# The sample's chunk of two pairs of heads as one unit of half A's RWKV recurrence

## Chip, core and metric

The kernel runs on one core of one Trainium2 chip. The metric is the device time of one execution in microseconds (us), the median of several runs. The engines are PE (TensorE, with PEld for its weight loads), DVE (VectorE), ACT (ScalarE), POOL (GpSimd) and SP (SyncE), whose queue issues nearly all DMAs of this kernel. Each engine works through its own instruction stream in order and waits on semaphores.

## What is computed

One inference step of a two-layer encoder trunk over 1024 prompt frames and 64 sample frames, in fp32. Layer 0 has a mixer of two kinds: RWKV-7 time mixing (8 heads of 64) and gated linear attention, GLA (4 heads); layer 1 has chunk-band attention; each layer has a SwiGLU. Prompt and sample go through the same weights, with states of their own. The change is in the RWKV mixer:

```
xs = pa + (prev - pa) * mu                      # token shift of the projected rows
r, k, v, xw, xa, xg = split(xs)
w = -softplus(-(w0 + tanh(xw) @ w2)) - 0.5;  decay = exp(-exp(w))
a = sigmoid(a0 + xa @ a2);  g = sigmoid(xg) @ g2
kk = normalised k * k_k;  k = k * (1 + (a - 1) * k_a)
S = S * w_t - (S kk_t) (kk_t a_t)^T + v_t k_t^T;  o_t = S r_t     # per head, frame after frame
y = (groupnorm(o) * ln_w + ln_b + sum(r k r_k) v) * g
...
mix = concat(ya, yb) @ w_out_mix
```

## The kernel before

**Halves and stages.** The 1088 frames are cut in two: half A is the first 384 prompt frames and the 64 sample frames (448 columns), half B the other 640 prompt frames. The program text goes: input projection of A for the RWKV part (`inproj_rwkv(0)`); recurrence of A, interleaved with the GLA units of A and the projection of A for the GLA part; loading of B's input (`load_xt(1)`) and B's projections (`inproj_gla(1)`, `inproj_rwkv(1)`); loading of A's mixer outputs (`load_xt(0, yg_d)`) and of the residual rows (`load_acc`, line 797); four steps of B's recurrence; A's output projection (`proj`, through `tsg`, evacuations in lines 825 to 829) with its layer norm (lines 887 to 905); the rest of B's recurrence; the first SwiGLU of A (`ffn(0, 0)`). Every GEMM of fp32 operands is made of three passes over high and low parts (lines 124 to 126, and 135 to 138), the parts split off by ACT (`wh`, `xh`) and by DVE or POOL (`wl`, `xl`).

**The recurrence.** It is worked in chunks of 64 frames. A unit holds one pair of heads (128 partitions) and `n` chunks. Half A has 16 units: first four for the sample, of one chunk each (pairs 0 to 3, 64 columns), and then 12 of two chunks each (three times four pairs, 128 columns). Half B has 20 units of two chunks. A unit goes through five stages: `rw1` (loads of `rkv`, `xg`, `rsb`; three small matmuls into `pa`; decay and keys), `rw1b` (`pb`: the chunk's 64x64 matrices; `lab`, line 487; the transposes into `pt`), `rw2` (the inverse of a triangular matrix: `lab` goes to DRAM, its 16x16 diagonal blocks come back as `lt` with `8*n` partitions, 15 pairs of tiny DVE instructions in lines 549 and 551 solve them, and the result goes through DRAM to `tt` and `t0`; then two levels of matmuls in `pz`), `rw3` (chunk after chunk: state and output, eight matmuls each in their dependence) and `rw4` (transposition, gate, store of `y` to `yg_d`, line 654). The generator `rwkv` lets five units be in flight, one in each stage. `pa`, `pb` and `pt` share one PSUM bank, `pz` has one; `lt`, `x16` and `bbk` have one buffer each.

**Order.** The instructions are ordered when the program is built: a planner simulates all engines with a cost model, takes among the ready instructions the one written earliest, and gives out buffers. The stream of each engine is therefore a mixture of recurrence, GEMM and filler, fixed beforehand; where a real duration differs from the planner's, the engine waits at the head of its stream.

**What the tail of A's recurrence feeds.** `load_xt(0, yg_d)` loads eight row blocks `yraw` (line 214), four from GLA and four from RWKV, and splits them (lines 215 and 216) into the tiles `xh`, `xl` of half A. These tiles lend part of their space to half B's input while B's projection runs (`xt_tiles_in`). The `yraw` buffers and the projection's temporary tiles are given up before `acc`, the residual rows, is loaded; `acc` lies in that space. Filler work, such as `cache_setup` (`cv`, `ck`, `cvh`, lines 1126 to 1132, casts by line 113) and the weight casts of line 101, stands in the same streams.

Of the kernel before, what the change touches and what calls it, by code (L numbers as in the profile page):

```python
# [10 lines left out]
F32 = mybir.dt.float32  # L11
F32R = mybir.dt.float32r
U8 = mybir.dt.uint8
AF = mybir.ActivationFunctionType
# [5 lines left out]
PA = 384  # L20
NA, NB = PA + 64, 1024 - PA
NM = max(NA, NB)
SMP = PA
# [60 lines left out]
class Kern:  # L84
# [324 lines left out]
        eng.tensor_tensor(dst, src.unsqueeze(2).to_broadcast([128, m, 2, 64]),  # L409
                          self.bd3.unsqueeze(1).to_broadcast([128, m, 2, 64]), op=ALU.mult)  # L410

    def rw1(self, sp, p, n, g0):

        nc, V, A, G, T = self.nc, self.V, self.A, self.G, self.T
        W = 64 * n
        u = SimpleNamespace(p=p, n=n)
        pc = slice(128 * p, 128 * p + 128)
# [7 lines left out]
        gs = slice(g0, g0 + W)  # L425
        rkv = sp.tile([128, 3, W], F32, tag="rkv", name="rkv", bufs=3)
        nc.sync.dma_start(rkv, self.rkv_d[:, p, :, gs].rearrange("a p t -> p a t"))
# [4 lines left out]
        for h in range(2):  # L432
            src = self.rs_d[2 * p + h : 2 * p + h + 1, gs]
            nc.sync.dma_start(rsb[QH[h]], bass.AP(tensor=src.tensor, offset=src.offset, ap=[[0, 64], [1, W]]))

        pa = self.sbank("pa")
        T.matmul(pa[:, 0:W], self.w2z[:, pc], xg[:, 0, :], start=True, stop=True)
        T.matmul(pa[:, W : 2 * W], self.a2z[:, pc], xg[:, 0, :], start=True, stop=True)
        T.matmul(pa[:, 2 * W : 3 * W], self.g2[:, pc], xg[:, 1, :], start=True, stop=True)
        th = st("th", bufs=2)  # L440
        A.activation(th, pa[:, 0:W], AF.Tanh, bias=self.w0h[:, p : p + 1], scale=0.5)
        tha = st("tha")
        A.activation(tha, pa[:, W : 2 * W], AF.Tanh, bias=self.a0h[:, p : p + 1], scale=0.5)
        u.gt = st("gt", bufs=5)
        A.copy(u.gt, pa[:, 2 * W : 3 * W])
        kkn = st("kkn")
        V.scalar_tensor_tensor(kkn, k, self.kk[:, p : p + 1], rsb, op0=ALU.mult, op1=ALU.mult)
# [17 lines left out]
        G.tensor_scalar(tha, tha, self.kah[:, p : p + 1], self.kah1[:, p : p + 1], op0=ALU.mult, op1=ALU.add)  # L465
        G.tensor_tensor(tha, tha, k, op=ALU.mult)
        V.scalar_tensor_tensor(th, r, self.rk[:, p : p + 1], tha, op0=ALU.mult, op1=ALU.mult)
        G.tensor_tensor(bk[:, :, 1, :], ch(tha), ch(enb), op=ALU.mult)
        u.v, u.th, u.eb3, u.ar, u.bk = v, th, eb3, ar, bk
        return u  # L470

    def rw1b(self, sp, u):

        V, A, G, T, p, n = self.V, self.A, self.G, self.T, u.p, u.n
# [123 lines left out]

    def rw3(self, sp, u, S):

        V, A, G, T, p, n = self.V, self.A, self.G, self.T, u.p, u.n
# [36 lines left out]
        for h in range(2):  # L638
# [4 lines left out]
        return S2  # L643

    def rw4(self, sp, u, y0):

        A, G, T, p, W = self.A, self.G, self.T, u.p, 64 * u.n
# [3 lines left out]
        A.activation(y, py[:, 0:W], AF.Identity, scale=self.lnw[:, p : p + 1], bias=self.lnb[:, p : p + 1])  # L651
        G.tensor_tensor(y, y, u.bon, op=ALU.add)
        G.tensor_tensor(y, y, u.gt, op=ALU.mult)
        self.nc.sync.dma_start(self.yg_d[p, :, y0 : y0 + W], y)

    def rwkv(self, hf, sp, n, src, S):

        units = [(p, n, 64 * c, 0) for c in range(0, (PA, NB)[hf] // 64, n) for p in range(4)]
        if hf == 0:
            units = [(p, 1, SMP, 1) for p in range(4)] + units  # L660
            S += [self.state(sp, p, self.a["wkv0"]) for p in range(4)]
        else:
            S += [self.state(sp, p, src) for p in range(4)]
        st = {}
        def one(i):
            p, m, c0, smp = units[i]
            st[i] = self.rw1(sp, p, m, self.base[hf] + c0)

        def three(i):
            p, m, c0, smp = units[i]  # L670
            S[p] = self.rw3(sp, st[i], S[p])
            if smp:
                self.wkv_out(sp, S[p], self.a["s_wkv"][2 * p : 2 * p + 2])
                S[p] = self.state(sp, p, src)
            elif hf == 0 and c0 == PA - 64 * n:
                self.nc.sync.dma_start(self.wkv_d[p].rearrange("(h k) v -> k h v", h=2), S[p])
# [917 lines left out]
```

## Time and profile before

| what | value |
|---|---|
| median of 3 runs | 3114.89 us (3114.37 to 3117.97) |
| the profiled execution's own time | 3118.8 us |
| its span, first to last instruction | 3117.0 us |
| mean granted TensorE clock | 0.978 |
| half A's recurrence, first `lab` to last store of `y` | 100.2 to 551.4 us |
| half B's recurrence, last store of `y` | 1117.7 us |

The profile page gives busy time by engine, slices of the span, the chain of work that ended last and the costliest groups of instructions. The views behind it are asked by stretch (busy time of every engine between two times), by line or tile (count, durations, first and last start), by waits, and as a timeline. In a timeline a row reads: start, duration, engine, line, operation, output and inputs, shapes, count, and in square brackets the idle time of the engine before it and what ended that. A PE row's duration contains a modelled tail, so the distance of two starts tells more of the pace than the duration does.

### The profile page before, as it was taken

To read this page: it belongs to the slowest core of one execution; us is meant where nothing else is said; L and a number is where in the kernel's file an instruction comes from. 1 tells how busy PE (TensorE), PEld (TensorE's weight loads), DVE (VectorE), ACT (ScalarE), POOL (GpSimd) and SP (SyncE) were. 2 spreads that over 40 slices of the span, in tenths; PEclk is the share of its full clock that TensorE was granted. 3 is DMA by queue.
4 is the path that set the end of the run, shared out by engine and by line. 5 is a ranking of instruction groups with operands and counts; after the bars stand their busy time and mean duration, and the time that the engine had idled before them with its cause. 6 is when DMAs were issued, how large, how long until landed. Compare 5 with 4: busy or idle time off the path is not lost.

```text
span 3117.0 us, 50050 instructions
## 1 busy us (share of the span) xinstructions
PE 3007.7 (96%) x17468; PEld 2672.1 (86%) x17468; DVE 2025.6 (65%) x4941; ACT 1271.7 (41%) x2761; POOL 1363.4 (44%) x1489
## 2 busy tenths in 40 slices
PE   8999999899999999999999999999999989799998
PEld 7878888688888888798999898899999968799987
DVE  5687875879898764555554556245666668666567
ACT  4454554344444334243343132355444433333332
POOL 2354533444554234343342233245555556645444
PEclk9999999889999999999999999999999999999999
DMA  6553334533533238344443223865445443322122
GB/s 200 142 161 113 109 111 122 147 104 107 148 113 103 83 105 296 106 155 123 121 123 100 75 102 116 255 186 172 137 144 150 122 160 108 108 80 96 65 82 75
DMA packets 298492, 399.29 MB, mean 128 GB/s; under 512 B 125504, under 2 KB 218552, under 8 KB 298240
## 3 DMA queue, kind: packets, MB, share of 16 engines
q1 hardware_dynamic: 297088, 393.48, 41.0%
q8 instruction: 138, 2.26, 0.3%
q10 hardware_dynamic: 1152, 2.62, 0.2%
q14 instruction: 114, 0.93, 0.1%
HBM read 323.63 MB, written 75.51 MB: 128 GB/s over the span
## 4 chain that ended last, share of the span: by engine, by line
PE 78%; DMA 7%; DVE 7%; POOL 3%; issue 2%; ACT 2%; SPq 1%; POOLq 0%; ACTq 0%; DVEq 0%
PE gps L124 11%; PE gps L126 11%; PE gps L125 11%; PE gps L135 8%; PE gps L136 8%; PE gps L138 7%; PE gps L1066 2%; PE gps L1067 2%; PE gps L1068 2%; PE op L1329 2%; PE tp L1303 2%; PE sps L1287 1%; PE sps L1288 1%; PE ps L622 1%; DVE x L551 1%
## 5 line engine op out<-in xcount | busy, mean ns | idle before, releaser
L108 POOL TENSOR_TENSOR wl<-wr,wh 128x512 fp32r<-128x512 f32 (+2 forms) x297 | 522.9, 1763 | 655.5 <-ACT wh L101 602.3
L124 PE MATMUL gps<-xh,wh 128*128 128x320 f32 (+1 forms) x2188 | 746.4, 341 | 8.5 <-ACT xh L215 5.8
L125 PE MATMUL gps<-xl,wh 128*128 128x320 f32 (+1 forms) x2188 | 745.9, 341 | 0.6 <-DVE xl L216 0.6
L126 PE MATMUL gps<-xh,wl 128*128 128x320 f32 (+1 forms) x2188 | 745.1, 341 | 0.2
L101 ACT CAST wh<-wr 128x1024 fp32r<-128x1024 f32 x360 | 375.9, 1048 | 465.8 <-PE gps L125 136.5
L106 DVE TENSOR_TENSOR wl<-wr,wh 128x512 fp32r<-128x512 f32 (+2 forms) x297 | 288.8, 973 | 252.2 <-ACT wh L101 249.1
L124 PEld LDWEIGHTS gps<-xh,wh 128*128 128x128 f32 x2188 | 415.0, 190 | 30.1 <-ACT xh L215 5.8
L126 PEld LDWEIGHTS gps<-xh,wl 128*128 128x128 f32 x2188 | 414.5, 189 | 18.6 <-POOL wl L108 1.2
L125 PEld LDWEIGHTS gps<-xl,wh 128*128 128x128 f32 x2188 | 414.5, 189 | 18.3 <-DVE xl L216 1.0
L1298 POOL TENSOR_SCALAR s<-s,mx 128x640 f32<-128x640 f32 (+5 forms) x144 | 203.0, 1410 | 277.2 <-DVE mx L1297 250.4
L135 PE MATMUL gps<-wh,xh 128*128 128x512 f32 x661 | 263.1, 403 | 9.2 <-ACT wh L101 3.8
L138 PE MATMUL gps<-wh,xl 128*128 128x512 f32 x661 | 259.2, 399 | 6.6 <-DVE xl L216 6.1
L136 PE MATMUL gps<-wl,xh 128*128 128x512 f32 x661 | 264.2, 401 | 0.4 <-DVE wl L106 0.2
L135 PE MATMUL gps<-wh,hh 128*128 128x512 f32 x572 | 226.7, 398 | 3.8 <-ACT xh L113 3.5
L136 PE MATMUL gps<-wl,hh 128*128 128x512 f32 x572 | 226.9, 398 | 0.0
L827 DVE TENSOR_TENSOR acc<-acc,gps 128x512 f32<-128x512 f32 x216 | 143.5, 679 | 84.8 <-PE gps L138 82.3
L138 PE MATMUL gps<-wh,hl 128*128 128x512 f32 x484 | 189.6, 397 | 1.3 <-DVE hl L946 1.1
L549 DVE TENSOR_TENSOR t<-lt,x 16x48 f32<-16x48 f32 (+9 forms) x540 | 151.2, 280 | 35.6 <-DMA lt<-l_d 25.2
L1296 ACT ACTIVATE s<-s,mx 128x640 f32<-128x640 f32 (+5 forms) x144 | 96.4, 670 | 161.2 <-DVE mx L1295 151.7
L135 PEld LDWEIGHTS gps<-wh,xh 128*128 128x128 f32 x661 | 126.5, 192 | 39.9 <-ACT wh L101 6.4
L138 PEld LDWEIGHTS gps<-wh,xl 128*128 128x128 f32 x661 | 126.0, 191 | 35.4 <-DVE xl L216 7.0
L136 PEld LDWEIGHTS gps<-wl,xh 128*128 128x128 f32 x661 | 126.7, 192 | 30.2 <-DVE wl L106 2.0
(380 smaller groups left out, 6308.3 us busy)
## 6 DMA issues: line engine op xcount, KB each, us to landing
wr<-in_w_fi SPq DMA_DIRECT2D x176, 512.0 KB
wr<-in_w_fo SPq DMA_DIRECT2D x88, 512.0 KB
wr<-in_w_in SPq DMA_DIRECT2D x44, 512.0 KB
wr<-in_w_qk SPq DMA_DIRECT2D x32, 512.0 KB
wr<-in_w_o SPq DMA_DIRECT2D x24, 512.0 KB
qs<-qd SPq DMA_DIRECT2D x32, 320.0 KB
wr<-in_w_om SPq DMA_DIRECT2D x16, 512.0 KB
wr<-in_w_v SPq DMA_DIRECT2D x16, 512.0 KB
```

Source lines behind the costliest of these rows:

```text
L101: self.A.copy(hi, raw)
L106: self.V.tensor_tensor(lo[:, :h], raw[:, :h], hi[:, :h].bitcast(F32), op=ALU.subtract)
L108: self.G.tensor_tensor(lo[:, h:], raw[:, h:], hi[:, h:].bitcast(F32), op=ALU.subtract)
L124: self.T.matmul(ps, hi[:, kt, :], xh, start=(kt == 0), stop=False)
L125: self.T.matmul(ps, hi[:, kt, :], xl, start=False, stop=False)
L126: self.T.matmul(ps, lo[:, kt, :], xh, start=False, stop=(kt == nk - 1))
L135: self.T.matmul(ps, xh, wh, start=(i == 0), stop=False)
L136: self.T.matmul(ps, xh, wl, start=False, stop=(lo is None and i == n - 1))
L138: self.T.matmul(ps, cols(lo(kt)), wh, start=False, stop=(i == n - 1))
L549: V.tensor_tensor(tv, lt[:, j, w:16].unsqueeze(2).to_broadcast([m, r, w]), x[:, 0, j, 0:w].unsqueeze(1).to_broadcast([m, r, w]), op=ALU.mult)
L827: self.V.tensor_tensor(a, a, ps[:m], op=ALU.add)
L1298: G.tensor_scalar(s[:m, :nk], s[:m, :nk], mx[:m, 3:4], None, op0=ALU.mult)
```

## The change

The four one-chunk units of the sample become two units that hold two pairs of heads each, (0, 1) and (2, 3): the second pair takes the place that a second chunk has in a prompt unit. Half A then has 14 units, all of them 128 columns wide and with 16 diagonal blocks in `rw2`. What differs by pair (matmuls with a pair's weights, per-partition constants, initial and final state, loads and stores) is done in a loop over `u.segs`; everything else is done once for both pairs. In `rw3` the two chunks are worked one after the other as before, but the state isn't handed on from one to the next. `rw1b` and `rw2` have the same text but for names. The loop over pairs has a single turn in all other units, and they issue the instructions that they did.

```diff
-    def rw1(self, sp, p, n, g0):
+    def rw1(self, sp, ps, n, g0):
...
-        W = 64 * n
-        u = SimpleNamespace(p=p, n=n)
+        w = 64 * n
+        W = w * len(ps)
+        n *= len(ps)
+        u = SimpleNamespace(n=n, segs=[(p, slice(w * i, w * i + w)) for i, p in enumerate(ps)])
...
-        nc.sync.dma_start(rkv, self.rkv_d[:, p, :, gs].rearrange("a p t -> p a t"))
+        for p, cs in u.segs:
+            nc.sync.dma_start(rkv[:, :, cs], self.rkv_d[:, p, :, gs].rearrange("a p t -> p a t"))
...
-        xg = sp.tile([128, 2, W], F32, tag="xg", name="xg", bufs=2)
+        xg = sp.tile([128, 2, w], F32, tag="xg", name="xg", bufs=2)
...
+        for p, cs in u.segs:
+            pc = slice(128 * p, 128 * p + 128)
+            for i, (m, x) in enumerate(((self.w2z, 0), (self.a2z, 0), (self.g2, 1))):
+                T.matmul(pa[:, W * i + cs.start : W * i + cs.stop], m[:, pc], xg[:, x, :], start=True, stop=True)
+        for p, cs in u.segs:
+            A.activation(th[:, cs], pa[:, cs], AF.Tanh, bias=self.w0h[:, p : p + 1], scale=0.5)
+            A.activation(tha[:, cs], pa[:, W + cs.start : W + cs.stop], AF.Tanh, bias=self.a0h[:, p : p + 1], scale=0.5)
         A.copy(u.gt, pa[:, 2 * W : 3 * W])
...
     def rw3(self, sp, u, S):
...
-        G.tensor_copy(u.sv[0:64, 0], S)
+        step = n // len(u.segs)
+        for i, (p, _) in enumerate(u.segs):
+            G.tensor_copy(u.sv[0:64, i * step], S[p])
+        out = {}
...
-            S2 = u.sv[0:64, c + 1] if c + 1 < n else sp.tile([64, 2, 64], F32, tag=f"S{p}", name="S", bufs=2)
+            p = u.segs[c // step][0]
+            if (c + 1) % step:
+                S2 = u.sv[0:64, c + 1]
+            else:
+                S2 = out[p] = sp.tile([64, 2, 64], F32, tag=f"S{p}", name="S", bufs=2)
...
     def rw4(self, sp, u, y0):
...
-        self.nc.sync.dma_start(self.yg_d[p, :, y0 : y0 + W], y)
+        for p, cs in u.segs:
+            self.nc.sync.dma_start(self.yg_d[p, :, y0 : y0 + cs.stop - cs.start], y[:, cs])
...
-        units = [(p, n, 64 * c, 0) for c in range(0, (PA, NB)[hf] // 64, n) for p in range(4)]
+        units = [((p,), n, 64 * c, 0) for c in range(0, (PA, NB)[hf] // 64, n) for p in range(4)]
         if hf == 0:
-            units = [(p, 1, SMP, 1) for p in range(4)] + units
+            units = [((p, p + 1), 1, SMP, 1) for p in (0, 2)] + units
```

More of the change, by code (lines that the diff above doesn't have):

```diff
@@ L423, in ch @@
             return t.rearrange("p (c s) -> p c s", c=n)
-        gs = slice(g0, g0 + W)
+        gs = slice(g0, g0 + w)
         rkv = sp.tile([128, 3, W], F32, tag="rkv", name="rkv", bufs=3)
-        nc.sync.dma_start(rkv, self.rkv_d[:, p, :, gs].rearrange("a p t -> p a t"))
+        for p, cs in u.segs:
+            nc.sync.dma_start(rkv[:, :, cs], self.rkv_d[:, p, :, gs].rearrange("a p t -> p a t"))
         r, k, v = rkv[:, 0, :], rkv[:, 1, :], rkv[:, 2, :]
-        xg = sp.tile([128, 2, W], F32, tag="xg", name="xg", bufs=2)
+        xg = sp.tile([128, 2, w], F32, tag="xg", name="xg", bufs=2)
@@ L430, in rw1 @@
         nc.sync.dma_start(xg, self.xg_d[:, :, gs].rearrange("a p t -> p a t"))
         rsb = st("rsb", bufs=2)
-        for h in range(2):
-            src = self.rs_d[2 * p + h : 2 * p + h + 1, gs]
-            nc.sync.dma_start(rsb[QH[h]], bass.AP(tensor=src.tensor, offset=src.offset, ap=[[0, 64], [1, W]]))
+        for p, cs in u.segs:
+            for h in range(2):
+                src = self.rs_d[2 * p + h : 2 * p + h + 1, gs]
+                nc.sync.dma_start(rsb[QH[h], cs], bass.AP(tensor=src.tensor, offset=src.offset, ap=[[0, 64], [1, w]]))
@@ L436, in rw1 @@
         pa = self.sbank("pa")
[L437 to L443, printed above, removed]
@@ L444, in rw1 @@
-        u.gt = st("gt", bufs=5)
+        th, tha, kkn = st("th", bufs=2), st("tha"), st("kkn")
+        u.gt = st("gt", bufs=5)
+        for p, cs in u.segs:
[5 more added lines that the diff above has]
+            A.activation(tha[:, cs], pa[:, W + cs.start : W + cs.stop], AF.Tanh, bias=self.a0h[:, p : p + 1], scale=0.5)
@@ L445, in rw1 @@
         A.copy(u.gt, pa[:, 2 * W : 3 * W])
-        kkn = st("kkn")
-        V.scalar_tensor_tensor(kkn, k, self.kk[:, p : p + 1], rsb, op0=ALU.mult, op1=ALU.mult)
+        for p, cs in u.segs:
+            V.scalar_tensor_tensor(kkn[:, cs], k[:, cs], self.kk[:, p : p + 1], rsb[:, cs], op0=ALU.mult, op1=ALU.mult)
         lw = st("lw", 65 * n)
@@ L464, in rw1 @@
         V.scalar_tensor_tensor(bk[:, :, 0, :], ch(kkn), 0.5, ch(enb), op0=ALU.mult, op1=ALU.mult)
-        G.tensor_scalar(tha, tha, self.kah[:, p : p + 1], self.kah1[:, p : p + 1], op0=ALU.mult, op1=ALU.add)
+        for p, cs in u.segs:
+            G.tensor_scalar(tha[:, cs], tha[:, cs], self.kah[:, p : p + 1], self.kah1[:, p : p + 1], op0=ALU.mult, op1=ALU.add)
         G.tensor_tensor(tha, tha, k, op=ALU.mult)
-        V.scalar_tensor_tensor(th, r, self.rk[:, p : p + 1], tha, op0=ALU.mult, op1=ALU.mult)
+        for p, cs in u.segs:
+            V.scalar_tensor_tensor(th[:, cs], r[:, cs], self.rk[:, p : p + 1], tha[:, cs], op0=ALU.mult, op1=ALU.mult)
         G.tensor_tensor(bk[:, :, 1, :], ch(tha), ch(enb), op=ALU.mult)
@@ L472, in rw1b @@
     def rw1b(self, sp, u):
-        V, A, G, T, p, n = self.V, self.A, self.G, self.T, u.p, u.n
+        V, A, G, T, n = self.V, self.A, self.G, self.T, u.n
         W = 64 * n
@@ L599, in rw3 @@
     def rw3(self, sp, u, S):
-        V, A, G, T, p, n = self.V, self.A, self.G, self.T, u.p, u.n
+        V, A, G, T, n = self.V, self.A, self.G, self.T, u.n
         W = 64 * n
@@ L642, in rw3 @@
             A.activation(on[:, hs], on[:, hs], AF.Identity, scale=rstd[:, h : h + 1], bias=m)
-        return S2
+        return out
     def rw4(self, sp, u, y0):
-        A, G, T, p, W = self.A, self.G, self.T, u.p, 64 * u.n
+        A, G, T, W = self.A, self.G, self.T, 64 * u.n
         py = self.sbank("py")
@@ L650, in rw4 @@
         y = sp.tile([128, W], F32, tag="y", name="y", bufs=1)
-        A.activation(y, py[:, 0:W], AF.Identity, scale=self.lnw[:, p : p + 1], bias=self.lnb[:, p : p + 1])
+        for p, cs in u.segs:
+            A.activation(y[:, cs], py[:, cs], AF.Identity, scale=self.lnw[:, p : p + 1], bias=self.lnb[:, p : p + 1])
         G.tensor_tensor(y, y, u.bon, op=ALU.add)
         G.tensor_tensor(y, y, u.gt, op=ALU.mult)
-        self.nc.sync.dma_start(self.yg_d[p, :, y0 : y0 + W], y)
+        for p, cs in u.segs:
+            self.nc.sync.dma_start(self.yg_d[p, :, y0 : y0 + cs.stop - cs.start], y[:, cs])
     def rwkv(self, hf, sp, n, src, S):
-        units = [(p, n, 64 * c, 0) for c in range(0, (PA, NB)[hf] // 64, n) for p in range(4)]
+        units = [((p,), n, 64 * c, 0) for c in range(0, (PA, NB)[hf] // 64, n) for p in range(4)]
         if hf == 0:
-            units = [(p, 1, SMP, 1) for p in range(4)] + units
+            units = [((p, p + 1), 1, SMP, 1) for p in (0, 2)] + units
             S += [self.state(sp, p, self.a["wkv0"]) for p in range(4)]
@@ L665, in one @@
         def one(i):
-            p, m, c0, smp = units[i]
-            st[i] = self.rw1(sp, p, m, self.base[hf] + c0)
+            ps, m, c0, smp = units[i]
+            st[i] = self.rw1(sp, ps, m, self.base[hf] + c0)
         def three(i):
[L670 to L676, printed above, removed]
+            ps, m, c0, smp = units[i]
+            for p, s in self.rw3(sp, st[i], S).items():
+                S[p] = s
+                if smp:
+                    self.wkv_out(sp, s, self.a["s_wkv"][2 * p : 2 * p + 2])
+                    S[p] = self.state(sp, p, src)
+                elif hf == 0 and c0 == PA - 64 * n:
+                    self.nc.sync.dma_start(self.wkv_d[p].rearrange("(h k) v -> k h v", h=2), s)
         for i in range(len(units) + 4):
```

1 line of the change is left out of this document (removed).

## The prediction

> **What bounds the kernel now.** I read the page first, for which engine carries the span and which carries the chain.
>
> ```profile
> span 3117.0 us, 50050 instructions
> PE 3007.7 (96%) x17468; PEld 2672.1 (86%) x17468; DVE 2025.6 (65%) x4941; ACT 1271.7 (41%) x2761; POOL 1363.4 (44%) x1489
> PE 78%; DMA 7%; DVE 7%; POOL 3%; issue 2%; ACT 2%; SPq 1%; POOLq 0%; ACTq 0%; DVEq 0%
> ```
>
> PE is busy for 96% of the span. So an instruction taken from another engine counts only where PE stands idle or runs at a low clock. Next I asked for the stretches around half A's recurrence (columns: stretch, length, then busy time and count for PE, PEld, DVE, ACT, POOL, then granted clock, DMA share, GB/s).
>
> ```profile
> 85.00:135.00 50.00, 48.38 (x241) 40.75 (x240) 31.08 (x123) 26.55 (x68) 20.19 (x35) 0.97 0.60 146
> 135.00:210.00 75.00, 68.80 (x390) 56.49 (x389) 59.51 (x161) 43.74 (x101) 39.41 (x58) 0.93 0.46 145
> 210.00:460.00 250.00, 244.72 (x1716) 215.15 (x1715) 203.38 (x744) 124.16 (x387) 109.94 (x211) 0.99 0.40 114
> 460.00:532.00 72.00, 72.00 (x536) 66.53 (x535) 40.35 (x140) 31.92 (x89) 24.96 (x47) 1.00 0.45 136
> 532.00:565.40 33.40, 18.93 (x83) 15.16 (x81) 18.97 (x63) 11.70 (x36) 11.50 (x19) 0.72 0.64 134
> 565.40:610.00 44.60, 44.60 (x224) 36.91 (x224) 42.96 (x102) 15.91 (x40) 21.11 (x26) 0.94 0.50 140
> 610.00:637.00 27.00, 20.83 (x106) 16.45 (x105) 25.36 (x62) 13.28 (x37) 19.93 (x26) 0.59 0.35 116
> 637.00:1118.00 481.00, 478.40 (x2936) 409.52 (x2936) 395.21 (x1253) 213.50 (x610) 215.71 (x338) 0.98 0.38 109
> ```
>
> From 85 to 532 us, where A's recurrence runs beside B's input projection, PE is idle for 1.6 + 6.2 + 5.3 + 0 = 13.1 of 447 us. From 637 us, with B's recurrence beside A's SwiGLU, it is idle for 2.6 of 481. Between them lies the one hole that A's recurrence reaches: 532 to 565.4 us, where PE does 18.9 of 33.4 us at clock 0.72. In the last step before 637 (layer norm) DVE is full, 25.4 of 27 us. So the question is how much of the hole the change closes. The timelines of PE, ACT, DVE and SP show what holds it open.
>
> ```profile
> 538.24 0.80 PE L138 MATMUL gps<-wh,xl 128*128 128x512 f32 x1 [4.84 <-DVE xl L216]
> 557.51 2.08 PE L484 MATMUL pb<-ar,bbk 128*128 128x128 f32 x8 [7.59 <-ACT gt L445]
> 565.36 0.77 PE L135 MATMUL gps<-wh,xpk 128*128 128x512 f32 x1 [0.47 <-POOL bk L468]
> ...
> 542.86 0.40 ACT L113 CAST cvh<-cv 128x256 fp32r<-128x256 f32 x1 [3.67 <-DMA cv<-in_ck_v]
> 556.37 0.40 ACT L113 CAST cvh<-cv 128x256 fp32r<-128x256 f32 x1 [11.42 <-DMA cv<-in_ck_v]
> 557.68 0.56 ACT L215 CAST xh<-yraw 128x448 fp32r<-128x448 f32 x1 [0.23 <-DMA yraw<-yg_d]
> ...
> 540.54 1.14 DVE L216 TENSOR_TENSOR xl<-yraw,xh 128x448 fp32r<-128x448 f32 x2
> 558.28 0.62 DVE L216 TENSOR_TENSOR xl<-yraw,xh 128x448 fp32r<-128x448 f32 x1 [0.28 <-ACT xh L215]
> 564.57 0.69 DVE L825 SCALAR_TENSOR_TENSOR acc<-acc,gps 128x512 f32<-128x512 f32 x1 [1.01 <-DMA acc<-in_x]
> ...
> 550.97 0.36 SPq L427 DMA_DIRECT2D rkv<-rkv_d  x1
> 551.42 0.44 SPq L654 DMA_DIRECT2D yg_d<-y  x1
> ...
> 555.10 0.32 SPq L214 DMA_DIRECT2D yraw<-yg_d  x1
> ...
> 558.93 1.82 SPq L797 DMA_DIRECT2D acc<-in_x  x4
> ```
>
> Read it backwards. PE resumes the output projection at 565.4 because its PSUM banks are full until DVE adds the first one to `acc` at 564.57, and DVE waits there for the load of `acc`. SP issues that load at 558.93, right after the last split of `yraw` ends on DVE (558.28 + 0.62 = 558.90): `acc` lies in space that `yraw` gives up. That split waits for the load at 555.10, and that for the store of A's last `y` at 551.42. So the last unit of A's recurrence is on the path. The other seven splits were over at 540.54 + 1.14 = 541.7.
>
> **The change, part by part.** *How much earlier A ends.* The sample's stages take the place of prompt stages, unit for unit.
>
> ```profile
> L487 DVE TENSOR_TENSOR lab<-pb,mab x16: 269/405/424, 100.2 to 458.8; 128x256 f32<-128x256 f32 x12, 128x128 f32<-128x128 f32 x4
> ...
> L487 DVE TENSOR_TENSOR lab<-pb,mab x14: 269/404/424, 100.2 to 405.5; 128x256 f32<-128x256 f32 x10, 128x128 f32<-128x128 f32 x4
> ```
>
> The sixteenth `lab` comes at 458.8 us, the fourteenth at 405.5. If a merged unit keeps a sample unit's pace, A ends 458.8 - 405.5 = 53 us earlier, and its last store moves from 551.4 to about 498. It may cost some of that, but 14 us are enough for the step below (until 541.7), so I need not know it better.
>
> *What is removed on DVE.* Two units' chains of tiny instructions go: 2 x 30, 250 to 290 ns each by their group, which is 15 to 17 us; some 36 wider ones become 18 of twice the size. All lie beside a PE that is busy, so I cost them at nothing; without that cover they would be a gain of up to 17 us more, never a loss. Of the DMAs, 7 per unit of `rw2` and one `xg` go twice, 16 issues.
>
> ```profile
> L551 DVE TENSOR_TENSOR x<-x,t 8x15 f32<-8x15 f32 (+7 forms) x47 | 13.8, 293 | 1.2
> L549 DVE TENSOR_TENSOR t<-lt,x 8x15 f32<-8x15 f32 (+7 forms) x47 | 11.8, 251 | 9.2 <-DMA lt<-l_d 8.1
> ...
> L510 PE MATMUL pt<-th,bdk x10: 221/275/275, 105.2 to 195.7; 128*128 128x64 f32 x8, 128*128 128x128 f32 x2
> ```
>
> *What is removed on PE.* Matmuls go by chunk and pair, and so stay, but for one with `bdk` and two transposes a unit. The first is 2 instructions: 8 narrow ones become 4 wide ones; of the transposes 4 go. Eight instructions of under 0.275 us overlap one another, so at most 2.2 us; I take **-1 us**, on the path because PE is.
>
> *What is moved.* The first four units of A, loads and stores included, are now all of full width, so DVE has about 10 us more of recurrence in front of the splits of B's input (estimate: some 2.5 us a unit for about fifteen instructions that double), and POOL and ACT likewise, between 100 and 210 us. PE gets matmuls of two more chunk-pairs there as well, which fill it. The bounds are 0, if they cover, and +6.2 us, all of PE's idle time in 135:210 once more. I take **+2 us**, nearer to 0, since the extra matmuls are cover.
>
> *The hole.* With A's last `y` early, all eight splits follow B's last projection matmul, and the eighth ends at 541.7 + 0.6 = 542.3. SP can then issue `acc`. How long it takes to land is the term with bounds far apart. In the trace it took 558.93 to 564.57, 5.6 us. But at 541 us the queue was slower, by this row of the chain:
>
> ```profile
> 540.47 10.45 DMA rkv_d<-xs
> ```
>
> A store issued at 540.47 landed only at 550.9, and the load of `rkv` at 550.97, which waits for it, held up everything behind it on SP. Best: 542.3 + 5.6 = 547.9, and PE resumes at 548.7 instead of 565.4, -16.7 us. Worst: `acc` stands behind that load, is issued at about 552 and used at 557.6, -7 us. I take 542.3 + 10.45 = 552.8, resumption 0.8 us later as now at 553.6, which is **-12 us**: the transfer of the same moment is the nearest row. What is late next is DVE, which is full from 565 to 637; it has 33.4 - 19.0 = 14.4 us idle in the hole, so 12 can be taken out of it without a queue of its own. After 637 PE is full and passes the shift on.
>
> Sum: -1 + 2 - 12 = **-11 us**. The profiled execution took 3118.8 us (1.8 around its span), 3.9 above the median; it would be 3107.8, and the median 3114.89 - 11 = **3104** us.
>
> **The rivals.** *Nothing comes of it (3114 us).* PE is full on both sides, the hole stays for another reason: the ACT wait of 11.42 us for `cv`, behind the same blocked SP queue, holds DVE and PE as well, and B's first units need data of the last projection tiles whatever A does. For it speaks that PE's own wait of 7.59 us is released by ACT and not by A. Against it, `acc` is issued within 0.1 us of the split. The Trainium skill ("Perfetto Trace Analysis", Identifying the Most-Contended Engine) says to work first on the engine with the highest occupancy; by that rule 20 us off DVE change nothing here and the time would be 3114 us. The trace agrees for 85:532 and 637:1118 and not for the hole.
>
> *The hole closes and stays warm (3095 us).* If `acc` lands in 5.6 us, PE has no gap after its first banks, -16.7. It also saves the slow pace after the gap: at clock 0.72 the 18.9 us of matmuls in the hole lose 0.28 x 18.9 = 5.3 us against clock 1.00; I count some 3 of them as saved. Sum -1 + 2 - 16.7 - 3, about -19 to -20. The skill's clock page ("TensorE: Matmul & The Clock Gate", Part 1) puts the return to full pace at about 3.4 us of busy array; by that figure one such stretch at half pace costs about 1.7 us, and the sum would be 1.3 us less.
>
> *Fillers move ahead into the projection (3126 us).* With A out of the way by 500 us, the planner has free places on ACT and SP between 490 and 532, and can put the six casts of `cv` and `ck` there, ahead of the weight casts that PE needs. Each waits at the head of ACT's stream for its load, 3.67 us in the milder of the two rows above. In a stretch where PE is idle for 0 of 72 us, six of them are 22 us; less the 11, +11. Three cancel the gain (3 x 3.67 = 11), five make it slower by more than can be missed. Against it: a bank of the projection is 24 matmuls, at 72 us for 536 instructions in 460:532 some 3.2 us, and PE has three banks, so a single wait of that length is mostly covered.
>
> **How the numbers follow.** A measurement of this kernel tells some 0.2%, 6.2 us, from no change. Chances: forecast (-16 to -6.2) 0.40, warm hole 0.13, nothing (within 6.2 either way) 0.25, fillers or another order that costs (+6 to +20) 0.22. So faster 0.53, same 0.25, slower 0.22. The likeliest one's own range is 3099 to 3108.7. The range for 8 in 10 has to hold the warm hole but for its last few us and half of the slower case: 3091 to 3125.
>
> **What would show it.** Right: 14 `lab` in half A; its last store of `y` before 541; `acc` issued at 541 to 546; PE's idle time between the end of B's projection and the layer norm down by about 8 us or more; the SwiGLU's first matmul at about 626 instead of 637. Wrong: `acc` still issued after 552 (nothing); waits for `cv` before 532 (fillers); PE idle time in 135:210 above 8 us (the moved units cost more than 2); or half B's recurrence ending after A's SwiGLU, which now has some 20 us to spare: it stores its last `y` at 1117.7, and the last hidden cast is at 1137.0.
>
> ```profile
> L944 ACT CAST hh<-ht x22: 550/562/580, 656.6 to 1137.0; 128x448 fp32r<-128x448 f32 x22
> ...
> L654 SPq DMA_DIRECT2D yg_d<-y x36: 319/396/1168, 187.6 to 1117.7; - x36
> ```

## The result, and the profile after

| | before | after |
|---|---|---|
| median of 4 runs each | 3116.43 us (3114.37 to 3120.23) | 3134.45 us (3133.37 to 3136.42) |
| profiled execution, and its span | 3118.8, 3117.0 us | 3136.42, 3134.6 us |

The ratio is 1.0061, 95% interval 1.0049 to 1.0073: the change costs 18 us where the prediction had a gain of 11. The page of the kernel after, its head and the shares of the chain:

```profile
span 3134.6 us, 49875 instructions
PE 3016.2 (96%) x17460; PEld 2677.2 (85%) x17460; DVE 1993.3 (64%) x4837; ACT 1266.7 (40%) x2731; POOL 1355.0 (43%) x1463
PE 73%; DVE 9%; DMA 9%; POOL 3%; issue 2%; ACT 2%; SPq 1%; POOLq 0%; DVEq 0%; ACTq 0%
```

DVE is busy 32 us less and 175 instructions are gone, as meant. The chain shows where to look: DMA has gone from 7% to 9%, PE from 78% to 73%. The same stretches up to 532 us as before (columns as in the prediction):

```profile
85.00:135.00 50.00, 42.36 (x191) 34.25 (x191) 24.93 (x73) 25.46 (x58) 21.93 (x31) 0.86 0.56 125
135.00:210.00 75.00, 70.85 (x399) 56.65 (x397) 49.95 (x165) 32.01 (x79) 27.83 (x39) 0.93 0.49 141
210.00:460.00 250.00, 240.61 (x1659) 208.23 (x1659) 194.50 (x716) 126.92 (x393) 118.88 (x215) 0.96 0.38 110
460.00:532.00 72.00, 70.53 (x497) 66.42 (x496) 34.29 (x101) 33.55 (x79) 23.80 (x40) 0.99 0.47 144
```

In 85:135 PE is idle for 7.6 us instead of 1.6, at clock 0.86 instead of 0.97, and does 191 matmuls instead of 241. Here time is lost first. The chain of the stretch from 90 to 112 us, then SP's and DVE's timelines, name the reason:

```profile
91.62 3.83 DMA rkv_d<-xs
...
95.47 10.55 DMA rkv<-rkv_d
...
106.04 0.28 DVE kkn L451
```

```profile
91.62 0.32 SPq L303 DMA_DIRECT2D rkv_d<-xs  x1
91.99 0.43 SPq L1394 DMA_DIRECT2D out_dram<-shS  x1
...
95.47 0.37 SPq L429 DMA_DIRECT2D rkv<-rkv_d  x1
...
106.04 0.28 DVE L451 SCALAR_TENSOR_TENSOR kkn<-rkv,vec,rsb 128x64 f32<-128x64 f32 x1 [10.55 <-DMA rkv<-rkv_d]
```

The second merged unit, pairs (2, 3), is now the second unit of all, and needs pair 3's columns as soon as A's projection has stored its last tile (91.62). Right behind that tile SP issues the store of the sample's shift state (`shS`, 14 x 128 single fp32 numbers, from [128, 14] to [14, 128]: 1792 pieces of 4 bytes). The load of pair 3, asked for at 95.47, lands 10.55 us later, and DVE, ACT and PE run dry behind `kkn`. Before, pair 3 was the fourth unit; SP loaded its `rkv` long after that store, and `kkn` didn't wait for it:

```profile
111.82 0.37 SPq L427 DMA_DIRECT2D rkv<-rkv_d  x1
...
117.63 0.28 DVE L447 SCALAR_TENSOR_TENSOR kkn<-rkv,vec,rsb 128x64 f32<-128x64 f32 x1
```

At the other end A's recurrence does finish early. The rows of `lab` and of the splits, then SP's timeline around the load of `acc`, what SP waited for there, and DVE's timeline:

```profile
L493 DVE TENSOR_TENSOR lab<-pb,mab x14: 383/406/415, 116.0 to 428.7; 128x256 f32<-128x256 f32 x14
...
L216 DVE TENSOR_TENSOR xl<-yraw,xh x8: 602/606/974, 550.4 to 560.3; 128x448 fp32r<-128x448 f32 x8
...
504.88 0.32 SPq L669 DMA_DIRECT2D yg_d<-y  x1
```

```profile
559.65 0.42 SPq L303 DMA_DIRECT2D rkv_d<-xs  x1
560.12 0.43 SPq L1395 DMA_DIRECT2D out_dram<-shP  x1
569.01 3.91 SPq L813 DMA_DIRECT2D acc<-in_x  x4
...
SPq L813 <- DMA rkv_d<-xs: 5.3, 1, 5.3
...
578.31 0.69 DVE L841 SCALAR_TENSOR_TENSOR acc<-acc,gps 128x512 f32<-128x512 f32 x1 [5.35 <-DMA acc<-in_x]
```

The last `y` goes out at 504.88 and the eighth split ends at 560.9, but `acc` is issued at 569.01. It is held by the store of the projection's last tile (559.65), which lands 9.3 us after its issue, at 568.99: the `xs` tiles, too, lie in the space that `acc` takes. And right behind that store goes the second store of single numbers, `shP`. `acc` itself then takes 9.3 us from its issue to its first use on DVE (578.31), near the 10.45 that the prediction took for it.

**Where the 18 us are.** To compare the kernels stage by stage, I cut PE's stream at the same matmuls of the large products (the 300th, 500th, 1700th and 2200th) and added up, in each piece, by how much the distance of two starts exceeds the median distance for the same form in the kernel before. What remains, PE's pure work, is 2813.0 us before and 2813.6 after. Lost PE time in us, from each run's profiled execution:

```
kernel                                  start  load  recurrence  hole   rest    sum
before                                   10.4   5.0     56.1     54.3  159.7  285.5
after                                     7.1  17.5     64.0     49.5  164.3  302.4
e1  after's text, nothing merged          7.0   4.1     59.1     53.7  159.2  283.1
e2  only (0, 1) merged                    7.5  12.0     69.4     54.4  158.1  301.4
e3  (2, 3) fourth                        10.0   9.7     56.8     45.5  161.5  283.6
e4  after, both shift stores later        8.8   7.8     59.4     39.5  174.9  290.4
e5  before, both shift stores later       8.2   2.0     57.5     49.2  171.4  288.3
e6  before, pair 3 second                 9.0  18.1     55.5     54.4  163.4  300.4
e7  e3, both shift stores later           7.9   1.8     56.0     42.6  175.6  283.9
e8  after, only shS later                 9.6   5.1     61.0     47.4  166.3  289.4
e9  after, stores on ScalarE's queue      6.9  17.2     63.7     50.7  164.5  302.9
e10 e3, stores on ScalarE's queue        10.3   5.6     53.0     46.1  160.9  276.0
e11 before, stores on ScalarE's queue     7.8   6.9     54.0     54.3  158.5  281.6
e12 after, stores as rows                 8.3   9.3     64.3     66.4  158.5  306.9
e13 before, stores as rows                7.5   4.4     56.8     57.1  154.8  280.6
e14 e3, stores as rows                    7.2   4.8     57.1     57.4  160.3  286.8
e15 e2, stores as rows                    8.4   7.2     68.1     60.3  157.1  301.1
e16 (2, 3) third                          7.1  12.3     61.3     51.5  161.3  293.4
e17 sixteen units in e3's order           9.5   3.5     68.1     50.5  160.8  292.4
```

Before, the pieces begin at 6, 80, 137, 513 and 709 us. From before to after: -3.3, +12.5, +7.9, -4.8, +4.6, in sum +16.9 of the spans' 17.6. The rows "before" and e1, which do the same work, differ by up to 3.4 us in a piece, so a difference of 3 or 4 us there is no evidence. Each row is a single run, and the runs of some kernels lie far apart (e2, e16 and e17 over 14 to 15 us). The row of e2 is its slowest run, 7.8 us over the median, those of e6 and e12 lie 4.5 and 4.9 over it, those of e8 and e10 4.1 and 3.2 under it. So the signs of the large differences count, not their last microseconds.

### The profile page after: what moved, and what is told of

It is laid out like the page before. It is cut to its first block, busy times and chain, and to the rows that moved or that the text cites. A ratio compares the mean times of both kernels' runs of the same rounds, so it can differ in the third digit from the quotient of the medians.

```text
span 3134.6 us, 49875 instructions
## 1 busy us (share of the span) xinstructions
PE 3016.2 (96%) x17460; PEld 2677.2 (85%) x17460; DVE 1993.3 (64%) x4837; ACT 1266.7 (40%) x2731; POOL 1355.0 (43%) x1463
## 4 chain that ended last, share of the span: by engine, by line
PE 73%; DVE 9%; DMA 9%; POOL 3%; issue 2%; ACT 2%; SPq 1%; POOLq 0%; DVEq 0%; ACTq 0%
PE gps L124 10%; PE gps L125 10%; PE gps L126 10%; PE gps L135 8%; PE gps L136 8%; PE gps L138 7%; PE gps L1082 2%; PE gps L1084 2%; PE gps L1083 2%; PE op L1345 2%; PE tp L1319 2%; DMA wr<-in_w_in 1%; DVE t L555 1%; DVE x L557 1%; PE sps L1303 1%
## 5 line engine op out<-in xcount | busy, mean ns | idle before, releaser
L125 PEld LDWEIGHTS gps<-xl,wh 128*128 128x128 f32 x2188 | 414.6, 189 | 18.5 <-DVE xl L216 1.0
L555 DVE TENSOR_TENSOR t<-lt,x 16x15 f32<-16x15 f32 (+7 forms) x510 | 129.3, 253 | 38.5 <-DMA lt<-l_d 28.4
```

The source lines that it names most:

```text
L125: self.T.matmul(ps, hi[:, kt, :], xl, start=False, stop=False)
L555: V.tensor_tensor(tv, lt[:, j, w:16].unsqueeze(2).to_broadcast([m, r, w]), x[:, 0, j, 0:w].unsqueeze(1).to_broadcast([m, r, w]), op=ALU.mult)
```

## The experiments

Each was timed in three to five rounds beside the kernel before on the same chip. The first four expectations speak of theory 1 (a load is late because of what is ahead of it) and of rivals: the rewritten text, and the width of the merged units. Times are medians; each ratio is to the kernel before of the same call, with its interval.

**e1: after's text with nothing merged.** Sixteen units again, all else as after.

```diff
-            units = [((p, p + 1), 1, SMP, 1) for p in (0, 2)] + units
+            units = [((p,), 1, SMP, 1) for p in range(4)] + units
```

> The changed text with four units of one pair for the sample again, so 16 units; the loops over pairs have one turn each. Theory T1 (the merged second unit needs pair 3's load before 100 us, that load lies in the DMA queue behind the 4-byte store of the shift row, and DVE, ACT and PE wait in order): no such wait, 3116 us within 4. Rival R1 (the rewritten text alone gives the planner another order, and that costs): 3125 to 3135. Rival R2 (wider first units put more work ahead of the splits of half B's input): 3116, since the units are narrow.

3116.0 us, ratio 0.9994 (0.9984 to 1.0005). The rewritten text costs nothing; what costs is the units.

**e2: only (0, 1) merged,** pairs 2 and 3 alone, fifteen units.

```diff
-            units = [((p, p + 1), 1, SMP, 1) for p in (0, 2)] + units
+            units = [(ps, 1, SMP, 1) for ps in ((0, 1), (2,), (3,))] + units
```

> Only pairs 0 and 1 are merged, pairs 2 and 3 are units of their own: 15 units. T1: pair 3 is asked for a stage later, its load is no longer waited for before 106 us; 3112 to 3120. R2: half of the extra width, half of the loss, some 3125. R1: as far from before as the changed kernel, 3128 to 3136.

3127.89 us, ratio 1.0031 (1.0016 to 1.0045), against what theory 1 expected; the number is nearer to the rival of the width (some 3125). But the early wait is there, though pair 3 is a narrow unit again. With one merged unit ahead pair 3 moves forward as well: its load is asked for at 93.17 us, right behind the store (90.94), and DVE waits for it:

```profile
105.90 1.21 DVE L451 SCALAR_TENSOR_TENSOR kkn<-rkv,vec,rsb 128x64 f32<-128x64 f32 x1 [8.52 <-DMA rkv<-rkv_d]
```

The table has 12.0 for the load, and 69.4, the highest of all, for the recurrence.

**e3: the second merged unit fourth,** behind the first two prompt units.

```diff
-            units = [((p, p + 1), 1, SMP, 1) for p in (0, 2)] + units
+            units = [((0, 1), 1, SMP, 1)] + units[:2] + [((2, 3), 1, SMP, 1)] + units[2:]
```

> Both merged units, but the one of pairs 2 and 3 stands behind the first two prompt units (pairs 0 and 1): 14 units, the same work. T1: pair 3's load has time, the early stall of some 12 us goes, what is left of the loss are 5 to 8 us: 3119 to 3125. R2: the first units are as wide as in the changed kernel, so no gain: 3131 to 3137.

3112.77 us, ratio 0.9986 (0.9976 to 0.9996): 22 us less than after, with the same fourteen units, and better than theory 1 expected (3119 to 3125). Width by itself is not the cost. The gain of the fourteen units is now seen in the hole, 45.5 against 54.3; the load piece is still above before (9.7 against 5.0).

**e4: after, with both shift stores held** until A's SwiGLU runs (issued at 704 and 857 us).

```diff
-        nc.sync.dma_start(a["s_shift"].rearrange("c p -> p c"), self.shS)
-        nc.sync.dma_start(a["p_shift"].rearrange("c p -> p c"), self.shP)
...
+            if j == 4:
+                with tc.issue_after(self.last_w):
+                    nc.sync.dma_start(a["s_shift"].rearrange("c p -> p c"), self.shS)
+            if j == 10:
+                with tc.issue_after(self.last_w):
+                    nc.sync.dma_start(a["p_shift"].rearrange("c p -> p c"), self.shP)
```

> The changed kernel with the stores of the two shift rows (14 x 128 single elements each) held back until the fifth and eleventh step of half A's SwiGLU; the SP queue ahead of the stall is otherwise the same. T1: the load of pair 3 issued at 95 us lands in 4 us instead of 10.5, and in the tail the last store of the projection lands in 3 to 4 us instead of 9.3, so that the residual rows come about 6 us earlier: 6 to 14 us faster than the changed kernel, 3120 to 3128. If the store is not what fills the queue: 3134 within 4.

3125.43 us, ratio 1.0026 (1.0015 to 1.0037). SP's and DVE's timelines now have `acc` issued right behind the landing of the projection's last tile:

```profile
547.10 0.41 SPq L303 DMA_DIRECT2D rkv_d<-xs  x1
551.75 1.86 SPq L813 DMA_DIRECT2D acc<-in_x  x4
...
557.38 0.69 DVE L841 SCALAR_TENSOR_TENSOR acc<-acc,gps 128x512 f32<-128x512 f32 x1 [0.42 <-DMA acc<-in_x]
```

4.7 us from store to `acc`, not 9.4, and DVE hardly waits. In the table load and hole fall by 9.7 and 10.0 against after, and the rest rises by 10.6. At its new place the first store meets half B's recurrence: the chain of 700 to 716 us has `rw2`'s small store landing after 9.63 us, against 2.15 for such a store in after (541.56), and PE stands idle for 6.5 of the 20 us from 700.

```profile
710.02 9.63 DMA t_d<-x
```

**e5: the same with the kernel before,** the control (the diff is e4's).

> The kernel before, with the two stores of the shift state moved out to the feed-forward part. Theory 1 (the store of single elements makes whatever is asked of its queue right behind it some 10 us late): in the kernel before nothing critical is asked behind the first store, since the load of pair 3 is issued only at 108.8 us, so nothing is gained early; behind the second store the last projection tile lands late (issued 540.47, 10.45 us), and acc is issued only then, so some 3 to 8 us are gained in the hole: ratio 0.9975 to 0.9990. Theory 2 (the store costs the same everywhere, whatever the order of units): the same gain as with the fourteen units, some 9 us, ratio 0.9970 or less. Theory 3 (the store is innocent): 0.9995 to 1.0005.

3123.97 us, ratio 1.0026 (1.0015 to 1.0036): slower, a miss for every theory, since none had counted the price at the new place (rest +11.7; load -3.0 and hole -5.1). (The load of pair 3 was issued at 111.82 us in before, not at 108.8.) Beside e4 it tells what fourteen units do when no store stands in their way: hole 39.5 against 49.2, so -9.7; load +5.8; in all the same time.

**e6: before, with pair 3 second.** Sixteen single units; only the load comes early.

```diff
-            units = [(p, 1, SMP, 1) for p in range(4)] + units
+            units = [(p, 1, SMP, 1) for p in (0, 3, 1, 2)] + units
```

> The kernel before with its sixteen units, but the sample's unit of pair 3 second instead of fourth, so that its load is asked for right behind the first store of single elements, as in the kernel after; no unit is merged. Theory 1 (the early load is what costs): the load takes 9 to 13 us to land, VectorE's kkn of that unit waits for it some 8 to 11 us, and the time goes up by 6 to 12 us, ratio 1.002 to 1.004. Theory 2 (it needs the wider units as well): within 2 us of before, ratio 0.9993 to 1.0007.

3129.35 us, ratio 1.0042 (1.0027 to 1.0057). DVE's timeline shows after's wait, with nothing merged:

```profile
108.09 0.28 DVE L447 SCALAR_TENSOR_TENSOR kkn<-rkv,vec,rsb 128x64 f32<-128x64 f32 x1 [9.47 <-DMA rkv<-rkv_d]
```

The load piece rises by 13.1 us, the time by 13, a little more than the 6 to 12 expected; the other pieces stay within 4. The early load alone costs what after loses there.

**e7: e3's order, with both shift stores held** as in e4.

> Fourteen units, the second merged one fourth, and both stores of the shift state held back to the feed-forward part. If the two gains seen so far are of different places (the order: no early wait; the stores: acc issued sooner in the hole) they add up in part: the early wait is gone already, so only the hole's 5 to 8 us come on top: ratio 0.9955 to 0.9975, some 3103 to 3109 us. If the order alone had freed the hole as well, nothing comes on top: ratio 0.998 to 0.999.

3116.83 us, ratio 1.0009 (0.9997 to 1.0021). A miss: load and hole lose less, but the rest more (175.6), as in e4 and e5.

**e8: after, with only the first store held,** e4's diff without its part for `p_shift`.

> The kernel after with only the first of the two shift stores held back; the second stays where it is. Of the 9 us that holding both gave, Theory 1 puts most at the early wait: the load of pair 3 lands in under 5 us, the early stall falls from some 12 us to 2 to 4, and acc is still issued at about 565 us (the last projection tile behind the second store): 3126 to 3130 us, ratio 1.003 to 1.0045. If the gain was the hole's alone: no change from the kernel after, ratio 1.0055 to 1.007.

3126.99 us, ratio 1.0029 (1.0019 to 1.004). As expected: 7.5 us of the 18 are won by the medians, some 10 by the ratios. The chain's row for the load, in place of 10.55 us:

```profile
92.90 2.83 DMA rkv<-rkv_d
```

The load piece is back at 5.1. What is left over the kernel before is 11 us by the medians and 4 by the profile, which fell on a faster run: 4.9 in the recurrence and 6.6 in the rest (where the store now lies), less 6.9 in the hole.

**e9, e10, e11: both stores issued on ScalarE's queue,** at their old places; e9 is after, e10 is e3, e11 is before.

```diff
-        nc.sync.dma_start(a["s_shift"].rearrange("c p -> p c"), self.shS)
-        nc.sync.dma_start(a["p_shift"].rearrange("c p -> p c"), self.shP)
+        nc.scalar.dma_start(a["s_shift"].rearrange("c p -> p c"), self.shS)
+        nc.scalar.dma_start(a["p_shift"].rearrange("c p -> p c"), self.shP)
```

> The kernel after with both shift stores at their old places in the program but issued on ScalarE's queue instead of SyncE's. Theory 1a (the store keeps the queue it is on): the load of pair 3 is no longer behind it and lands in 3 to 5 us, the early stall falls to 1 to 4 us, acc is issued at about 545 to 555 us, and, since no other queue has to carry the store later, all of it counts: 13 us early and some 5 in the hole, 3112 to 3119 us, ratio 0.999 to 1.001. Theory 1b (the store keeps the DMA engines, whichever queue it is on): the load still takes 9 us or more to land, 3130 to 3136 us, ratio 1.0045 to 1.0065.

> Fourteen units with the second merged one fourth (3112.8 us), and both shift stores issued on ScalarE's queue. Nothing waits long behind the first store in that order, so only the hole changes. Theory 1a: acc is issued 5 to 8 us sooner, 3105 to 3109 us, ratio 0.996 to 0.998. Theory 1b: unchanged, ratio 0.998 to 0.9995.

> The kernel before with both shift stores on ScalarE's queue: what the move of the stores gives where nothing critical is behind the first. Theory 1a: 3 to 8 us in the hole and the few us of the stage from 108 us, 3107 to 3112 us, ratio 0.997 to 0.9985. Theory 1b: 3115 to 3118 us, ratio 0.9995 to 1.0005. The gap of this to the kernel after with the same stores is what the fourteen units cost beside the stores: Theory 1a puts it at 3 to 8 us, from the row of late waits at 363 to 447 us.

e9: 3133.04 us, ratio 1.0044 (1.0026 to 1.0062). The chain of e9, then the stretch 92:104 of e9, of after and of e8 (where the store is elsewhere):

```profile
94.84 9.03 DMA rkv<-rkv_d
```

```profile
92.00:104.00 12.00, 11.53 (x31) 8.58 (x32) 2.56 (x8) 2.69 (x9) 2.37 (x6) 0.60 0.77 83
```

```profile
92.00:104.00 12.00, 11.25 (x35) 7.96 (x34) 2.90 (x8) 2.74 (x9) 2.41 (x6) 0.72 0.82 50
```

```profile
92.00:104.00 12.00, 12.00 (x62) 10.29 (x62) 6.47 (x18) 9.82 (x25) 6.83 (x14) 1.00 0.32 103
```

The load waits nearly as long with the store on another queue, as theory 1b has it. So it is not SP's queue that makes it late. The DMA engines are busy for 0.77 (e9) and 0.82 (after) of these 12 us and move 83 and 50 GB/s; without the store they are busy for 0.32 at 103 GB/s. The Trainium skill ("DMA: Bandwidth & Descriptors", Issuing engines are not separate DMA queues) says that transfers of all issuing engines run on the same 16 DMA engines and interleave; this trace agrees, with 9.03 us in e9 against 10.55 in after.

e10: 3110.43 us, ratio 0.9981 (0.997 to 0.9992), **better than both kernels**; that is theory 1b's range (unchanged against e3, 0.9976 to 0.9996), not theory 1a's 3105 to 3109. e11: 3113.45 us, 0.9992 (0.9983 to 1.0002), between the two theories. So fourteen units in a good order stand some 3 us below sixteen with the same stores (the two intervals overlap), and after's order 20 us above.

**e12 to e15: the stores as 14 rows of 512 bytes,** each after one transposition on PE; e12 is after, e13 before, e14 e3, e15 e2.

```diff
+    def shift_out(self, dst, sh, rw):
+        ps = self.tpsum()
+        self.T.transpose(ps[0:14, 0:128], sh, self.ident)
+        self.V.tensor_copy(rw, ps[0:14, 0:128])
+        self.nc.sync.dma_start(dst, rw)
...
-        nc.sync.dma_start(a["s_shift"].rearrange("c p -> p c"), self.shS)
-        nc.sync.dma_start(a["p_shift"].rearrange("c p -> p c"), self.shP)
+        self.shift_out(a["s_shift"], self.shS, one.tile([128, NM], F32, tag="sq", name="rwS", bufs=3)[:14, :128])
+        self.shift_out(a["p_shift"], self.shP, one.tile([128, NM], F32, tag="sq", name="rwP", bufs=3)[:14, :128])
```

> The kernel after, with each shift state transposed on TensorE and stored as 14 rows of 512 bytes, at the same places and on the same queue. Theory 1 (1792 pieces of 4 bytes are what makes the load of pair 3 late): it lands in under 5 us, the early stall falls from 13 us to 1 to 4, acc is issued 5 us sooner; 11 to 18 us less than the kernel after, 3116 to 3123 us, ratio 1.000 to 1.0025. Rival (the two loads and the weights on the queue are slow by themselves, the store only happens to lie there): 3129 to 3135 us, ratio 1.0045 to 1.006.

> The kernel before with the same two stores as rows: the control. Nothing critical waits behind the first store there, so only the hole gives: 2 to 8 us less than before, 3108 to 3114 us, ratio 0.9975 to 0.9993. What the kernel after with rows stands above this one is the fourteen units' own cost: Theory 1, from the late waits, 4 to 10 us; if all of it was the store, under 2 us or below.

> Fourteen units with the second merged one fourth, and the stores as rows. The first store's slowing of the stage from 95 to 110 us (6 us of lost time in this order) and that of the hole are both gone: 6 to 12 us less than that order alone, 3101 to 3107 us, ratio 0.995 to 0.997; if the stores cost nothing in this order, 3110 to 3113 us, ratio 0.998 to 0.999.

> Fifteen units (pairs 0 and 1 merged, 2 and 3 alone), stores as rows. The profile of that order showed 7 us of early loss and some 14 us of late waits at 349 to 497 us. If the late waits cost by themselves: 5 to 12 us above the kernel before with rows, 3115 to 3122 us; if they only take up time that is waited elsewhere anyway: within 3 us of it, 3107 to 3114 us.

e12: 3137.39 us, ratio 1.0068 (1.0055 to 1.0082). e13: 3118.38, 1.0 (0.9991 to 1.001). e14: 3117.78, 1.0006 (0.9996 to 1.0016). e15: 3136.22, 1.0062 (1.0049 to 1.0075). By their times all four are misses. The mechanism held: in e12 the load of pair 3, issued behind no such store, lands in a quarter of the time, as the chain has it,

```profile
95.46 2.67 DMA rkv<-rkv_d
```

and the load piece falls from 17.5 to 9.3 us. But the hole rises from 49.5 to 66.4. There PE has a transposition more in its fixed stream and all instructions behind it stand in another order; which of them costs the 17 us I didn't trace, and so these four tell nothing of the whole. They do show again that the fourteen units lose in the recurrence in after's order, 64.3 against 56.8 in e13, and not in e3's, 57.1 in e14.

**e16: the second merged unit third,** and **e17: e3's order with nothing merged.**

```diff
-            units = [((0, 1), 1, SMP, 1)] + units[:2] + [((2, 3), 1, SMP, 1)] + units[2:]
+            units = [((0, 1), 1, SMP, 1)] + units[:1] + [((2, 3), 1, SMP, 1)] + units[1:]
```

```diff
-            units = [((0, 1), 1, SMP, 1)] + units[:2] + [((2, 3), 1, SMP, 1)] + units[2:]
+            units = [((p,), 1, SMP, 1) for p in (0, 1)] + units[:2] + [((p,), 1, SMP, 1) for p in (2, 3)] + units[2:]
```

> Fourteen units, the second merged one third instead of second or fourth. Theory 1 (what costs is that the second merged unit's load is asked for while the first shift store is under way): one stage later its load is asked for at about 105 to 112 us, after that store has landed (103.8 us); no long wait for it; 3112 to 3119 us, ratio 0.9985 to 1.001. Rival (the merged units side by side cost by their width wherever they stand, and fourth only spreads them): between the two, 3119 to 3128 us, ratio 1.001 to 1.004.

> Sixteen units, nothing merged: the sample's pairs 0 and 1, the first two prompt units, then the sample's pairs 2 and 3. If the gain of 4 us in the order with the second merged unit fourth is the merging's, this is the kernel before within 2 us: ratio 0.9993 to 1.0007. If it is the order's: ratio 0.998 to 0.999.

e16: 3126.61 us, ratio 1.003 (1.0018 to 1.0042), the rival's number but not for its reason. SP asks for the load no later than in after:

```profile
92.46 0.39 SPq L1394 DMA_DIRECT2D out_dram<-shS  x1
...
95.04 0.37 SPq L429 DMA_DIRECT2D rkv<-rkv_d  x1
```

so the planner, and not the unit's turn, sets that time, and one place later was not late enough (load 12.3).

e17: 3129.42 us, ratio 1.0035 (1.0022 to 1.0048), against both expectations: e3's order without the merging is 13 us slower than before, with no late load (3.5), the loss in the recurrence (68.1 against 56.1). So the merging gains in that order 15 us by the ratios of e3 and e17 (17 by the medians), and in after's order it loses 18.

## Why the prediction was wrong

**What bounds the kernel: right, and not enough.** PE's pure work stayed at 2813 us, and the result is lost PE time. The rule of the Trainium skill that the prediction weighed ("Perfetto Trace Analysis", Identifying the Most-Contended Engine) had no change for 20 us off DVE; DVE lost 32 us and the time rose by 18, so the rule names the bound here but not the outcome.

**Removed on PE, -1: not found.** Work after less work before is +0.6 us. Nothing hangs on it.

**"What is moved", +2 us with bounds 0 and +6.2: the step that failed.** I counted the instructions that the first units issue, and bounded them by PE's idle time in 135:210. That stretch did behave (4.2 us idle). I didn't follow the one load that comes two units earlier, through the queue to what lies ahead of it. It cost +12.5 us in the piece before, from 80 us on; e6 shows 13.1 for the load alone, e8 shows 12.4 of it gone with the store away. The row of the store at 91 us stood in the trace of before. The chain's row of 10.45 us for a tile's store at 540, which the prediction itself quotes, was the same thing at the other end: there `shP` is issued right behind it (541.03), and with `shP` away the tile's store holds `acc` for 4.7 us alone (e4). I took it for the state of the queue and didn't ask what made it.

**The recurrence beside B's projection, taken as hidden: +8 us.** DVE's removed instructions were to lie beside a busy PE, as they do; but the units' order against the projection's matmuls was changed too. The whole piece, in before and then in after (columns as in the prediction):

```profile
137.00:513.00 376.00, 364.51 (x2487) 318.33 (x2486) 292.19 (x1011) 191.92 (x557) 165.93 (x300) 0.98 0.42 124
149.00:533.00 384.00, 370.75 (x2497) 322.29 (x2496) 272.03 (x955) 189.29 (x541) 168.82 (x291) 0.96 0.42 122
```

PE's idle time grows only from 11.5 to 13.3 us. What grows is the slow pace: a clock of 0.98 over 376 us loses some 7.5 us and 0.96 over 384 us some 15.4 (an estimate, as the clock has two digits), which is about the 8. Single waits are short: the longest between 330 and 465 us is 1.1 us in before and 2.1 in after.

The piece goes from 53 to 69 over the orders tried, high with sixteen units (e17) as with fifteen (e2). Neither the width nor the order sets it alone: e3 and e17 have the same order, and with the merging it is 56.8, without it 68.1. Why one stream is good and another bad is open: each build has another stream on every engine, and no run held the rest of the stream fixed.

**The hole, -12: -4.8.** That A would be early enough was right (504.88, against a limit of 541). That the eighth split would follow the projection's last matmul was right too (560.9). "SP can then issue `acc`" was wrong: I had the last split of `yraw` as what frees the space, since in before `acc` was issued within 0.1 us of its end. The space also holds the projection's `xs` tiles, as the description of the kernel says, and the prediction left that condition out. In before the last `xs` tile had been stored by 550.9, 8 us ahead of the split, so it didn't show; in after it is what comes last. This comes out near the sum's own worst case (`acc` behind that same slow store, -7): from the store of the last tile to `acc` it was 18.5 us before and is 9.4 after. Where `shP` is away, the fourteen units do win the hole: -9.7 us between e5 and e4. So the mechanism was right in its first half, and the second shift store kept it from paying.

**The other signs.** No wait for `cv` before 532 (its first load is at 548.9). So the slower case, to which the prediction gave 0.22, came by an order that costs and not by the fillers, and it came out above the range's 3125. PE's idle time in the 69 us behind the projection's last tile fell from 9.6 us (541 to 610, before) to 7.6 (560 to 629, after), not by 8. The SwiGLU's first matmul is at 658.5, against 637.0 before and 626 predicted. Half B's recurrence still ends ahead of A's SwiGLU:

```profile
658.47 1.48 PE L124 MATMUL gps<-xh,wh 128*128 128x448 f32 x3
...
L960 ACT CAST hh<-ht x22: 549/563/568, 677.7 to 1150.8; 128x448 fp32r<-128x448 f32 x22
...
L669 SPq DMA_DIRECT2D yg_d<-y x36: 320/343/689, 215.1 to 1118.9; - x36
```

## What to carry to other kernels

When units of work are merged or put in another order, follow each one's loads and not only its arithmetic: write down when the load is asked for now, when it will be, and what is in the DMA engines at that moment. A store of single numbers is worth looking for first: here it delayed the loads beside it from either of the two queues tried, and moving it to a place without slack only moved the loss. In this kernel, whose streams are fixed beforehand, the orders tried lie from 6 us below the kernel before to 18 us above it, so a merging should be tried in several orders before it is judged: here the same fourteen units gave 3134 and 3113 us.

## What the runs showed of the hardware

**A store of 7 KB takes 12 us and slows what is beside it.** The 1792 pieces of 4 bytes, as the chain of e10 has the store:

```profile
91.58 11.89 DMA out_dram<-shS
```

The load of pair 3 beside it took 9 to 13 us (10.55 in after, 9.03 from another queue in e9, 12.7 to its use in e2), against 2.7 to 2.8 us without it (e12, e8). In before, a load of weights issued right behind the store took 13.52 us, and the next of its kind 4.35:

```profile
91.89 13.52 DMA wr<-in_w_gv
...
107.45 4.35 DMA wr<-in_w_gv
```

**The half clock outlasts a short gap by far.** Stretches of 2 us in e12 (columns as before):

```profile
90.00:92.00 2.00, 0.42 (x3) 0.00 (x0) 0.49 (x1) 2.00 (x6) 0.98 (x1) 1.00 0.68 215
92.00:94.00 2.00, 1.49 (x9) 1.50 (x9) 1.79 (x7) 0.45 (x3) 1.67 (x2) 0.72 0.67 240
94.00:96.00 2.00, 2.00 (x7) 1.47 (x7) 1.87 (x7) 1.71 (x7) 0.99 (x3) 0.50 0.86 279
96.00:98.00 2.00, 2.00 (x4) 0.53 (x2) 0.89 (x2) 0.82 (x3) 1.43 (x4) 0.50 0.67 210
98.00:100.00 2.00, 2.00 (x6) 1.59 (x6) 1.84 (x5) 1.28 (x6) 0.46 (x1) 0.50 0.09 25
100.00:102.00 2.00, 2.00 (x7) 1.78 (x6) 0.86 (x2) 1.97 (x3) 0.87 (x3) 0.50 0.12 33
102.00:104.00 2.00, 2.00 (x8) 1.81 (x8) 0.07 (x1) 1.97 (x4) 1.17 (x2) 0.72 0.00 0
```

PE's timeline of the same stretch shows one gap, and how far apart the starts of the same matmul are at half and at full pace (0.37 and 0.20 us):

```profile
92.51 0.43 PE L451 MATMUL pa<-xg,w2z 128*128 128x64 f32 x2 [2.09 <-ACT gt L455]
...
98.24 0.74 PE L124 MATMUL gps<-xh,wh 128*128 128x448 f32 x1
...
102.14 0.57 PE L125 MATMUL gps<-xl,wh 128*128 128x448 f32 x1
102.51 0.57 PE L126 MATMUL gps<-xh,wl 128*128 128x448 f32 x1
...
103.19 0.36 PE L125 MATMUL gps<-xl,wh 128*128 128x448 f32 x1
103.39 0.37 PE L126 MATMUL gps<-xh,wl 128*128 128x448 f32 x1
```

PE is idle for 2.09 us and then runs at 0.50 for over 8 us, though by these rows it is busy all the time. At half pace 8 us of work lose 4 (an estimate), twice the gap. The prediction quoted the Trainium skill's clock page ("TensorE: Matmul & The Clock Gate", Part 1) for some 3.4 us of busy array until the full clock is back. From the first matmul of 128x448 on (98.24) it is 5 us here; those ahead of it are small ones (64 columns, or 32 rows), and no run shows whether they count as busy. In before, a gap of 1.47 us ends at 111.81, matmuls of 128x448 follow from 112.89, and their starts are 0.37 us apart until 116.29 and 0.20 from 116.57 on: some 3.5 us. That agrees with the Trainium skill's figure. So a wait of PE can be worth more than its own length in this kernel.
